# Modulation rows made in thirds, and a row norm whose root is taken on VectorE

## The chip, the cores and the metric

The program runs on one core of a Trainium2 chip. TensorE (PE, with its weight loads PEld), VectorE (DVE), ScalarE (ACT) and GpSimd (POOL) compute; SyncE (SP) issues all DMAs. The metric is the device time of one execution in microseconds, the median of several runs.

## What is computed

Two transformer blocks follow each other on 256 tokens of width 1024; the second block has two layers and, in its first layer, 256 context tokens beside them. All is in 32 bits.

```python
x = x + 0.5 * swiglu(rms_norm(x, ffn1_norm), ffn1_w_in, ffn1_w_out)      # first block
h = rms_norm(x, mix_norm)                                                # RWKV-7 and dilated attention on h @ w_in
x = x + merged @ w_out
x = x + 0.5 * swiglu(rms_norm(x, ffn2_norm), ffn2_w_in, ffn2_w_out)
for l in range(2):                                                       # second block
    ml = split(silu(c) @ w_ada[l] + b_ada[l], 6)                         # six modulation rows of 1024, same for the context
    hl = rmsnorm(xl, norm_g[l, 0]) * (1 + ml[1]) + ml[0]
    yl, yc = mixer(hl, hc, ...)                                          # mLSTM, differential attention, Fourier, merge, w_out
    xl = xl + ml[2] * yl
    xl = xl + ml[5] * swiglu(rmsnorm(xl, norm_g[l, 1]) * (1 + ml[4]) + ml[3], w_ffn_in[l], w_ffn_out[l])
return rmsnorm(xl, final_g)
```

`rms_norm(x, g)` is `x * rsqrt(mean(x*x) + 1e-6) * g`.

## The kernel before

Tokens lie in tiles `X[t]` of 128 rows (t is 0 and 1 for the tokens, 2 and 3 for the context). A product streams its weights through `weights` (L181 to L204): SP loads a 512 KB tile `wr`, ACT casts it to the high part `wh` (L202), DVE takes the low part `wl` (L203), and PE makes three products of each pair (L214 to L216, or L249 to L251 where the weights stand still). Four `wr` and three `wh`/`wl` buffers rotate, so the stream runs a few tiles ahead.

The program is written in one order, and a planner at build time puts each engine's instructions into a list by that order and by its own estimate of when each is ready; later work with its inputs there is pulled ahead into a gap, so an engine's list isn't the written order. On the chip every engine goes through its list in order.

**Modulation.** `ada(l, c0, c1)` makes the columns c0 to c1 of the modulation rows of layer l in steps: a step is 128 rows of `w_ada` by 512 columns (one 256 KB load `wa`, two multiply-adds `aa` on DVE, L1134), eight steps are a chunk, and a chunk is closed by a finish (`finish`, L1114 to L1122): PE sums over the partitions with a column of ones, ACT copies the two rows out, SP writes them to memory. The finish of a chunk is called in the second step of the next one. Four `aa` buffers hold two chunks for both streams. Each weight tile adds `rate` to a counter in `weights`, and each whole unit of it runs one step; what is left of the steps when a feed-forward ends is run there in a loop (`for it in (self.side, self.fine)`). Before, layer 0's 96 steps stand in two halves: 48 in the first feed-forward and 48 in the second of the first block, each at 0.4 a tile over its 66 tiles (the first four tiles of the first feed-forward go by before the generator starts). Layer 1's 96 steps stand in the feed-forward of layer 0, at 1.5 a tile.

**The norm.** `norm_steps` (L334) multiplies a tile by the gain (L338, 1024 columns on DVE); `rms_row` (L326) has ACT sum the squares of the whole row (L330); the mean (L331) and the inverse root (`rsqrt` with n = 1: L286, L290, and three rounds of L292 and L293) go on POOL, nine small instructions one behind the other; DVE then scales each half (L344, or L346 with the shift), PE turns it (L317), and ACT and DVE split it for the next product (L304, L305). `later` queues the second part of a norm, and `tick` and `need` run it between the tiles of a product. The norm of a tile begins when both column halves of its residual (`updates`, L459 or L462 and L463) are added. `outgoing` (L433) runs the last product of a stage, by column halves and groups of tiles, and calls the norm for each group.

**The end.** `last` (L1595): per tile, y = X times gain (L1602), the norm's root on POOL, y times root (L1604), one 512 KB store (L1605).

**Layer 0 of the second block.** `second_layer` (L1520): three branches; after each its gates (`gate_chunk`, eight weight tiles of 4 x 256 for the 1024 columns) and a projection; then `last_projection` with `w_out`, then the feed-forward. The Fourier branch's two products have four weight tiles each. mLSTM and differential attention run inside a pool of their own (`inner`), their gates and all of the Fourier branch outside one.

Of the kernel before, what the change touches and what calls it, by code (L numbers as in the profile page):

```python
# [10 lines left out]
F32 = mybir.dt.float32  # L11
# [120 lines left out]
class Builder:  # L132
    def __init__(self, ctx, tc, a):
# [9 lines left out]
        self.pending, self.credit = [], 0  # L143
# [136 lines left out]
    def rsqrt(self, m, n, name):  # L280

        nc = self.nc
        eng = nc.gpsimd if n == 1 else nc.vector
        y = self.s(n, name + "_y")
        w = self.s(n, name + "_w")
        eng.tensor_scalar(out=y.bitcast(I32), in0=m.bitcast(I32), scalar1=-0.5, scalar2=float(0x5F3759DF),  # L286
                                op0=ALU.mult, op1=ALU.add)
# [38 lines left out]
    def rms_row(self, x, name="rn"):  # L326
        nc = self.nc
        junk = self.q([P, D], F32, "junk")
        ss = self.s(1, name + "_s")
        nc.scalar.activation(out=junk, in_=x, func=AF.Square, accum_out=ss)  # L330
        nc.gpsimd.tensor_scalar(out=ss, in0=ss, scalar1=1.0 / D, scalar2=1e-6, op0=ALU.mult, op1=ALU.add)  # L331
        return self.rsqrt(ss, 1, name)

    def norm_steps(self, xT, t, x, gain, shift):  # L334
# [3 lines left out]
        nc.vector.tensor_tensor(out=hn, in0=x, in1=gain, op=ALU.mult)  # L338
        r = self.rms_row(x)
        yield  # L340
        for c in range(0, D, 512):
            v = hn[:, c:c + 512]
            if shift is None:
                nc.vector.tensor_scalar(out=v, in0=v, scalar1=r[:, 0:1], scalar2=None, op0=ALU.mult)  # L344
            else:
                nc.vector.scalar_tensor_tensor(out=v, in0=v, scalar=r[:, 0:1], in1=shift[:, c:c + 512], op0=ALU.mult,  # L346
                                               op1=ALU.add)
            self.to_split(v, 4, xT, c // P, t)
            yield
# [20 lines left out]
    def ffn(self, X, xT, groups, w_in, w_out, scale, gates, nxt):  # L370
# [9 lines left out]
        for k0, kn in FF_PARTS:  # L380
# [32 lines left out]
            else:  # L413
                self.outgoing(aT, kn, W, groups, res, nxt())
# [18 lines left out]
    def outgoing(self, xT, nk, W, groups, res, done):  # L433


        whole = lambda g: [(t, 0, 512) for t in g]
        if len(groups[0]) > 1:
# [547 lines left out]
    def last_projection(self, yT, nk, W, w, gates, M, first, w_out, groups, res, nxt):  # L985
# [7 lines left out]
        self.outgoing(mT, KD, [[(w_out, 0, c * 512, 512)] for c in range(2)], groups, res, nxt())  # L993

    def first_block(self, X, nxt):
# [17 lines left out]
        def side():  # L1013
# [3 lines left out]
            self.fine, self.rate = self.ada(0, 0, 3 * D), 0.4  # L1017
# [49 lines left out]
        self.last_projection(yT, KD, a["w_proj_rwkv"][0], 256, lambda c0: gate(c0 // 256), M, False, a["w_out"][0], groups,  # L1067
# [3 lines left out]
        with self.inner() as self.ip:  # L1071
            self.fine, self.rate = self.ada(0, 3 * D, 6 * D), 0.4
# [447 lines left out]
    def second_layer(self, l, X, xT, nxt):  # L1520
# [17 lines left out]
        for b, (fn, wb) in enumerate((("mlstm", "w_br_ml_2"), ("diffattn", "w_br_da_2"), ("fourier", "w_br_fn_2"))):  # L1538
            yT = SplitT(self, KD, w)
            if fn == "fourier":  # L1540
                self.fourier(xT, W, outs, yT)
# [4 lines left out]
            gate = lambda c0: [g for c in range(c0, c0 + n, 256) for g in self.gate_chunk(xT, W, U_GATE + b * D + c, w)]  # L1546
            gates = {c0: gate(c0) for c0 in range(0, D, n)}
# [101 lines left out]
```

## Time and profile before

| | us |
|---|---|
| median of 3 runs (2996.62 to 3001.39) | 2996.85 |
| the profiled execution | 3002.16 |
| its span, first to last instruction | 3000.4 |

A busy matmul row lasts longer than it holds up the next one, since matmuls overlap; the distance from one start to the next is what a matmul costs. The granted clock is given as a share of 2.4 GHz: 1.00 is the high level, 0.50 the low one, and values between are windows that saw both. "L" and a number is a line of the kernel. An entry such as [2.45 <-DVE hn L346] is the idle time of the engine just before the instruction and what ended it.

### The profile page before, as it was taken

How to read it: one execution, taken by the hardware profiler on the slowest of the kernel's cores; microseconds unless marked ns; L12 is line 12 of the kernel's file. 1: busy time of each engine (PE TensorE's matmuls, PEld its weight loads, DVE VectorE, ACT ScalarE, POOL GpSimd, SP SyncE). 2: the span in 40 equal slices, each digit the busy share in tenths (PEclk: the TensorE clock that was granted, in tenths of full speed). 3: DMA queues.
4: the chain of work that ended last, by engine and by line, in shares of the span. 5: the costliest groups of instructions: out<-in, count | busy, mean ns of one | idle time of the engine just before them, and what ended most of it. 6: DMA issues, size and time to landing. Idle time of an engine off the chain costs nothing.

```text
span 3000.4 us, 42489 instructions
## 1 busy us (share of the span) xinstructions
PE 2866.2 (96%) x16536; PEld 2436.1 (81%) x16536; DVE 1895.7 (63%) x3228; ACT 1186.0 (40%) x1955; POOL 123.9 (4%) x278
## 2 busy tenths in 40 slices
PE   8988899988998999999999999999999999999998
PEld 7976787777996888987788977877778897799797
DVE  7776958576767455436674266677664555665655
ACT  4434334234443344225442333222344444444443
POOL 1020000002002000000000001000020000000000
PEclk9999979679999999999999999999999999999999
DMA  8766535055674222231233355554442243255564
GB/s 266 222 200 205 169 97 147 32 180 186 211 222 130 67 67 64 75 103 50 64 124 99 88 165 150 159 173 151 155 134 85 85 139 102 78 152 169 168 188 142
DMA packets 298356, 409.59 MB, mean 137 GB/s; under 512 B 31525, under 2 KB 182949, under 8 KB 298154
## 3 DMA queue, kind: packets, MB, share of 16 engines
q1 hardware_dynamic: 298154, 406.87, 44.5%
q8 instruction: 130, 2.13, 0.3%
q14 instruction: 72, 0.59, 0.1%
HBM read 396.98 MB, written 3.24 MB: 133 GB/s over the span
## 4 chain that ended last, share of the span: by engine, by line
PE 80%; DVE 10%; issue 3%; ACT 3%; POOL 2%; DMA 1%; SPq 0%; ACTq 0%; POOLq 0%; DVEq 0%
PE g L215 11%; PE g L216 11%; PE g L214 11%; PE g L249 11%; PE g L251 10%; PE g L250 10%; DVE wl L203 2%; PE dC L1342 2%; PE tr L317 1%; PE I L1318 1%; DVE aa L1134 1%; PE pf L818 1%; ACT dae L1439 1%; PE pf L820 1%; PE f L1509 1%
## 5 line engine op out<-in xcount | busy, mean ns | idle before, releaser
L203 DVE TENSOR_TENSOR wl<-wr,wh 128x1024 fp32r<-128x1024 f32 (+1 forms) x606 | 733.5, 1212 | 630.7 <-ACT wh L202 628.8
L202 ACT CAST wh<-wr 128x1024 fp32r<-128x1024 f32 (+1 forms) x606 | 631.2, 1042 | 1056.2 <-PE g L216 515.6
L215 PE MATMUL g<-wl,xh 128*128 128x512 f32 (+2 forms) x1880 | 733.2, 390 | 13.0 <-DVE wl L203 13.0
L214 PE MATMUL g<-wh,xh 128*128 128x512 f32 (+2 forms) x1880 | 730.0, 391 | 4.4 <-ACT wh L202 2.1
L216 PE MATMUL g<-wh,xl 128*128 128x512 f32 (+2 forms) x1880 | 728.3, 388 | 0.1
L249 PE MATMUL g<-xh,wh 128*128 128x256 f32 (+1 forms) x2352 | 725.9, 309 | 2.2 <-DVE gate L981 1.5
L251 PE MATMUL g<-xh,wl 128*128 128x256 f32 (+1 forms) x2352 | 723.2, 308 | 2.3 <-DVE wl L203 2.3
L250 PE MATMUL g<-xl,wh 128*128 128x256 f32 (+1 forms) x2352 | 722.3, 307 | 0.0
L249 PEld LDWEIGHTS g<-xh,wh 128*128 128x128 f32 x2352 | 452.9, 193 | 33.2 <-issue 7.0
L251 PEld LDWEIGHTS g<-xh,wl 128*128 128x128 f32 x2352 | 453.0, 193 | 25.8 <-DVE wl L203 2.9
L250 PEld LDWEIGHTS g<-xl,wh 128*128 128x128 f32 x2352 | 452.8, 193 | 20.7 <-issue 1.3
L215 PEld LDWEIGHTS g<-wl,xh 128*128 128x128 f32 x1880 | 359.3, 191 | 88.0 <-DVE wl L203 19.5
L214 PEld LDWEIGHTS g<-wh,xh 128*128 128x128 f32 x1880 | 356.6, 190 | 84.1 <-issue 7.5
L216 PEld LDWEIGHTS g<-wh,xl 128*128 128x128 f32 x1880 | 359.4, 191 | 70.5 <-DVE xl L305 1.5
L1134 DVE SCALAR_TENSOR_TENSOR aa<-wa,cond,aa 128x512 f32<-128x512 f32 x336 | 231.9, 745 | 4.8 <-DMA wa<-in_w_ada_dram 4.7
L304 ACT CAST xh<-tr 128x256 fp32r<-128x256 f32 (+1 forms) x114 | 50.4, 463 | 119.8 <-PE tr L317 107.0
L1439 ACT ACTIVATE dae<-sc,dast 128x512 f32<-128x512 f32 (+1 forms) x96 | 58.5, 614 | 42.2 <-DVE dast L1437 37.3
L305 DVE TENSOR_TENSOR xl<-tr,xh 128x256 fp32r<-128x256 f32 (+1 forms) x114 | 57.4, 531 | 18.8 <-ACT xh L304 18.4
L1437 DVE TENSOR_REDUCE dast<-sc 128x1 f32<-128x512 f32 (+1 forms) x96 | 53.8, 597 | 24.2 <-PE sc L1436 23.8
L317 PE MATMUL tr<-ident,hn 128*128 128x128 f32 x160 | 28.5, 315 | 34.1 <-DVE hn L344 17.6
L317 PEld LDWEIGHTS tr<-ident,hn 128*128 128x128 f32 x160 | 22.1, 163 | 43.1 <-DVE hn L344 18.4
L1119 PE MATMUL ada<-aa,one 128*1 128x512 f32 x96 | 30.6, 646 | 27.7 <-DVE aa L1134 27.6
(386 smaller groups left out, 2693.9 us busy)
## 6 DMA issues: line engine op xcount, KB each, us to landing
wr<-in_w_in_dram SPq DMA_DIRECT2D x156, 512.0 KB
wa<-in_w_ada_dram SPq DMA_DIRECT2D x192, 256.0 KB
wr<-in_ffn_w_in_dram SPq DMA_DIRECT2D x88, 512.0 KB
wr<-in_w_ffn_in_dram SPq DMA_DIRECT2D x84, 512.0 KB
wr<-in_w_in_dram SPq DMA_DIRECT2D x156, 256.0 KB
wr<-in_w_ffn_out_dram SPq DMA_DIRECT2D x50, 512.0 KB
wr<-in_ffn_w_out_dram SPq DMA_DIRECT2D x44, 512.0 KB
wr<-in_w_out_dram SPq DMA_DIRECT2D x32, 512.0 KB
```

Source lines behind the costliest of these rows:

```text
L202: nc.scalar.copy(out=wh[:, :kn, :ntot], in_=src)
L203: nc.vector.tensor_tensor(out=wl[:, :kn, :ntot], in0=src, in1=wh[:, :kn, :ntot].bitcast(F32), op=ALU.subtract)
L214: nc.tensor.matmul(o_, xh, wh[:, n0:n1], start=(kc == 0), stop=False)
L215: nc.tensor.matmul(o_, xh, wl[:, n0:n1], start=False, stop=False)
L216: nc.tensor.matmul(o_, xl, wh[:, n0:n1], start=False, stop=(kc == nk - 1))
L249: nc.tensor.matmul(o_, wh[:, fs], xh, start=(kc == 0), stop=False)
L250: nc.tensor.matmul(o_, wh[:, fs], xl, start=False, stop=False)
L251: nc.tensor.matmul(o_, wl[:, fs], xh, start=False, stop=(kc == nk - 1))
L317: self.nc.tensor.transpose(p[:, j * P:(j + 1) * P], src[:, (c + j) * P:(c + j + 1) * P], self.ident)
L1134: nc.vector.scalar_tensor_tensor(out=y, in0=raw, scalar=self.cond[:, k, s:s + 1], in1=acc[s], op0=ALU.mult, op1=ALU.add)
L1342: nc.tensor.matmul(pc[:, 0:257], kw[:, kc * P:(kc + 1) * P], V[t][:, 0:257], start=True, stop=True)
L1439: nc.scalar.activation(out=em, in_=ps[:, 0:n], func=AF.Exp, bias=st[:, m:m + 1], scale=1.0, accum_out=st[:, 2 + m:3 + m])
```

## The change

Layer 0's modulation rows are made in three parts of 32 steps: columns 0 to 2D in the first feed-forward and 2D to 4D in the second, both at 0.6 steps a tile, and 4D to 6D in the Fourier branch and its gates of layer 0, in a pool of their own, at 1.4 a tile, with a loop behind the gates for what is left.

The norm: ACT sums the squares of the first 512 columns as soon as the first column half of the residual is added (`first_half`); DVE squares and sums the other 512, and DVE also takes the root, with the factor -0.5 folded in, so that eight small instructions follow the two sums. With a shift the gain is multiplied in two halves; without one, gain and root go in with one operation per half. The end's store goes out in two halves. In the other branches the gates move inside the pool.

```diff
     def rsqrt(self, m, n, name):
-        eng = nc.gpsimd if n == 1 else nc.vector
...
-        if n == 1:
-            h = self.s(1, name + "_h")
-            eng.tensor_scalar(out=h, in0=m, scalar1=-0.5, scalar2=None, op0=ALU.mult)
-            for _ in range(3):
-                eng.tensor_scalar(out=w, in0=y, scalar1=y[:, 0:1], scalar2=h[:, 0:1], op0=ALU.mult, op1=ALU.mult)
-                eng.tensor_scalar(out=y, in0=w, scalar1=1.5, scalar2=y[:, 0:1], op0=ALU.add, op1=ALU.mult)
-            return y
...
-    def rms_row(self, x, name="rn"):
+    def first_half(self, t, x):
         nc = self.nc
-        junk = self.q([P, D], F32, "junk")
-        ss = self.s(1, name + "_s")
-        nc.scalar.activation(out=junk, in_=x, func=AF.Square, accum_out=ss)
-        nc.gpsimd.tensor_scalar(out=ss, in0=ss, scalar1=1.0 / D, scalar2=1e-6, op0=ALU.mult, op1=ALU.add)
-        return self.rsqrt(ss, 1, name)
+        a = self.sums[t] = self.s(1, "rn_a", bufs=4)
+        nc.scalar.activation(out=self.h([P, 512], F32, "junk"), in_=x[:, 0:512], func=AF.Square, accum_out=a)
+        nc.vector.tensor_scalar(out=a, in0=a, scalar1=-0.5 / D, scalar2=-0.5e-6, op0=ALU.mult, op1=ALU.add)
+
+    def rms(self, t, x, junk):
+        nc = self.nc
+        if t not in self.sums:
+            self.first_half(t, x)
+        a = self.sums.pop(t)
+        h, y, w = self.s(1, "rn_h"), self.s(1, "rn_y"), self.s(1, "rn_w")
+        nc.vector.scalar_tensor_tensor(out=junk, in0=x[:, 512:D], scalar=1.0, in1=x[:, 512:D], op0=ALU.mult,
+                                       op1=ALU.mult, accum_out=h)
+        nc.vector.tensor_scalar(out=h, in0=h, scalar1=-0.5 / D, scalar2=a[:, 0:1], op0=ALU.mult, op1=ALU.add)
+        nc.vector.tensor_scalar(out=y.bitcast(I32), in0=h.bitcast(I32), scalar1=-0.5,
+                                scalar2=float(0x5F3759DF - 0x400000 - 0x40000000), op0=ALU.mult, op1=ALU.add)
+        for _ in range(3):
+            nc.vector.tensor_scalar(out=w, in0=y, scalar1=y[:, 0:1], scalar2=h[:, 0:1], op0=ALU.mult, op1=ALU.mult)
+            nc.vector.tensor_scalar(out=y, in0=w, scalar1=1.5, scalar2=y[:, 0:1], op0=ALU.add, op1=ALU.mult)
+        return y
 
     def norm_steps(self, xT, t, x, gain, shift):
         hn = self.q([P, D], F32, "hn")
-        nc.vector.tensor_tensor(out=hn, in0=x, in1=gain, op=ALU.mult)
-        r = self.rms_row(x)
+        half = lambda v, c: v[:, c:c + 512]
+        if shift is not None:
+            nc.vector.tensor_tensor(out=half(hn, 0), in0=half(x, 0), in1=half(gain, 0), op=ALU.mult)
+        r = self.rms(t, x, half(hn, 512))
+        if shift is not None:
+            nc.vector.tensor_tensor(out=half(hn, 512), in0=half(x, 512), in1=half(gain, 512), op=ALU.mult)
         yield
         for c in range(0, D, 512):
-            v = hn[:, c:c + 512]
+            v = half(hn, c)
             if shift is None:
-                nc.vector.tensor_scalar(out=v, in0=v, scalar1=r[:, 0:1], scalar2=None, op0=ALU.mult)
+                nc.vector.scalar_tensor_tensor(out=v, in0=half(x, c), scalar=r[:, 0:1], in1=half(gain, c), op0=ALU.mult,
+                                               op1=ALU.mult)
...
-    def outgoing(self, xT, nk, W, groups, res, done):
+    def outgoing(self, X, xT, nk, W, groups, res, done):
...
                 for c in range(2):
                     res(g, c, self.gemm(xT, nk, W[c], whole(g)))
+                    if c == 0:
+                        begin(g)
                 done(g)
         else:
             toks = [t for g in groups for t in g]
             res(toks, 0, self.gemm(xT, nk, W[0], whole(toks)))
+            begin(toks)
...
-            self.fine, self.rate = self.ada(0, 0, 3 * D), 0.4
+            self.fine, self.rate = self.ada(0, 0, 2 * D), 0.6
...
-            self.fine, self.rate = self.ada(0, 3 * D, 6 * D), 0.4
+            self.fine, self.rate = self.ada(0, 2 * D, 4 * D), 0.6
...
             if fn == "fourier":
-                self.fourier(xT, W, outs, yT)
+                with self.inner() as self.ip:
+                    if need_ctx:
+                        self.fine, self.rate = self.ada(0, 4 * D, 6 * D), 1.4
+                    self.fourier(xT, W, outs, yT)
+                    gates = {c0: gate(c0) for c0 in range(0, D, n)}
+                    for _ in self.fine:
+                        pass
...
-                    nc.vector.tensor_tensor(out=y, in0=X[t], in1=g, op=ALU.mult)
-                    r = self.rms_row(X[t], "fin")
-                    nc.vector.tensor_scalar(out=y, in0=y, scalar1=r[:, 0:1], scalar2=None, op0=ALU.mult)
-                    nc.sync.dma_start(out=out[0, t * P:(t + 1) * P, :], in_=y)
+                    r = self.rms(t, X[t], y[:, 512:D])
+                    for c in range(0, D, 512):
+                        nc.vector.scalar_tensor_tensor(out=y[:, c:c + 512], in0=X[t][:, c:c + 512], scalar=r[:, 0:1],
+                                                       in1=g[:, c:c + 512], op0=ALU.mult, op1=ALU.mult)
+                        nc.sync.dma_start(out=out[0, t * P:(t + 1) * P, c:c + 512], in_=y[:, c:c + 512])
```

`begin(g)` calls `first_half` for each tile of g.

## Rows read from the trace of the kernel before

**Rows 1.** The page, part 1: busy time of each engine over the whole span.
```profile
PE 2866.2 (96%) x16536; PEld 2436.1 (81%) x16536; DVE 1895.7 (63%) x3228; ACT 1186.0 (40%) x1955; POOL 123.9 (4%) x278
```
**Rows 2.** Windows: length; busy us PE, PEld, DVE, ACT, POOL; clock; DMA; GB/s.
```profile
207.60:238.00 30.40, 8.68 (x28) 2.21 (x28) 25.94 (x40) 6.96 (x13) 14.11 (x19) 0.61 0.52 151
238.00:245.00 7.00, 6.92 (x54) 6.89 (x54) 4.78 (x7) 4.69 (x8) 0.00 (x0) 1.00 0.25 71
909.60:931.70 22.10, 13.58 (x34) 6.22 (x33) 22.10 (x31) 4.84 (x8) 18.98 (x17) 0.77 0.66 214
```
**Rows 3.** The same for the multiply-adds of L1134: VectorE us (count), clock, DMA.
```profile
12.00:204.00 192.00, 44.86 (x64) 1.00 0.76 234
204.00:238.00 34.00, 21.45 (x32) 0.65 0.47 137
...
901.00:932.00 31.00, 21.80 (x32) 0.83 0.68 217
1540.00:1585.00 45.00, 21.72 (x32) 1.00 0.74 229
```
**Rows 4.** Waits of TensorE over the span: who for whom, us, times, longest.
```profile
PE ada L1119 <- DVE aa L1134: 27.6, 3, 13.2
```
**Rows 5.** TensorE in order of time, a finish in a stream: start, length.
```profile
1915.92 0.39 PE L250 MATMUL g<-xl,wh 128*128 128x512 f32 x1
1916.15 0.39 PE L251 MATMUL g<-xh,wl 128*128 128x512 f32 x1
1916.47 1.03 PE L1119 MATMUL ada<-aa,one 128*1 128x512 f32 x4
1917.42 0.50 PE L214 MATMUL g<-wh,xh 128*128 128x512 f32 x1
```
**Rows 6.** In order of time, the norm between w_out and the second feed-forward.
```profile
701.28 0.69 DVE L459 SCALAR_TENSOR_TENSOR X<-g,X 128x512 f32<-128x512 f32 x1 [0.16 <-PE g L216]
...
708.57 1.11 PE L317 MATMUL tr<-ident,hn 128*128 128x128 f32 x4 [5.51 <-DVE hn L344]
```
**Rows 7.** TensorE in order of time, at later norms and at its end.
```profile
1798.67 0.66 PE L317 MATMUL tr<-ident,hn 128*128 128x128 f32 x4 [2.45 <-DVE hn L346]
...
2192.83 1.12 PE L317 MATMUL tr<-ident,hn 128*128 128x128 f32 x4 [2.17 <-DVE hn L346]
...
2794.08 1.12 PE L317 MATMUL tr<-ident,hn 128*128 128x128 f32 x4 [5.98 <-DVE hn L346]
...
2986.85 0.39 PE L216 MATMUL g<-wh,xl 128*128 128x512 f32 x1
```
**Rows 8.** In order of time at the start: first cast, first product.
```profile
9.42 1.05 ACT L202 CAST wh<-wr 128x1024 fp32r<-128x1024 f32 x1 [0.42 <-DMA wr<-in_ffn_w_in_dram]
...
14.42 0.78 PE L214 MATMUL g<-wh,xh 128*128 128x512 f32 x1
```
**Rows 9.** The chain that ended last, its last 16 us: start, length, what.
```profile
2985.08 1.16 ACT junk L330 x2
...
2990.28 0.61 DVE rs L462
...
2996.07 0.76 DVE y L1604
```
**Rows 10.** Groups of VectorE instructions: count, busy, mean, idle before.
```profile
L346 DVE SCALAR_TENSOR_TENSOR hn<-hn,rn_y,mod 128x512 f32<-128x512 f32 x28 | 20.3, 746 | 26.1 <-POOL rn_y L293 26.1
L459 DVE SCALAR_TENSOR_TENSOR X<-g,X 128x512 f32<-128x512 f32 x28 | 18.3, 684 | 1.9 <-PE g L216 1.9
...
L297 DVE SCALAR_TENSOR_TENSOR dars_w<-dars_w,dams 128x4 f32<-128x4 f32 x36 | 5.3, 157 | 0.1
```
**Rows 11.** Windows: Fourier branch, its gates; a VectorE row behind a late load.
```profile
1628.00:1685.00 57.00, 57.00 (x336) 49.70 (x335) 17.35 (x28) 20.80 (x33) 0.00 (x0) 1.00 0.17 48
1685.00:1733.00 48.00, 48.00 (x372) 46.69 (x371) 11.91 (x11) 14.33 (x18) 0.00 (x0) 1.00 0.43 131
...
1558.12 4.73 DVE L1134 SCALAR_TENSOR_TENSOR aa<-wa,cond,aa 128x512 f32<-128x512 f32 x7 [2.67 <-DMA wa<-in_w_ada_dram]
```

More of the change, by code (lines that the diff above doesn't have):

```diff
@@ L282, in rsqrt @@
         nc = self.nc
[L283 removed]
         y = self.s(n, name + "_y")
         w = self.s(n, name + "_w")
[L286 removed]
+        nc.vector.tensor_scalar(out=y.bitcast(I32), in0=m.bitcast(I32), scalar1=-0.5, scalar2=float(0x5F3759DF),
                                 op0=ALU.mult, op1=ALU.add)
[L288 to L294 removed]
         for _ in range(3):
@@ L337, in norm_steps @@
         hn = self.q([P, D], F32, "hn")
-        nc.vector.tensor_tensor(out=hn, in0=x, in1=gain, op=ALU.mult)
-        r = self.rms_row(x)
+        half = lambda v, c: v[:, c:c + 512]
[4 more added lines that the diff above has]
+            nc.vector.tensor_tensor(out=half(hn, 512), in0=half(x, 512), in1=half(gain, 512), op=ALU.mult)
         yield
         for c in range(0, D, 512):
-            v = hn[:, c:c + 512]
+            v = half(hn, c)
             if shift is None:
-                nc.vector.tensor_scalar(out=v, in0=v, scalar1=r[:, 0:1], scalar2=None, op0=ALU.mult)
+                nc.vector.scalar_tensor_tensor(out=v, in0=half(x, c), scalar=r[:, 0:1], in1=half(gain, c), op0=ALU.mult,
+                                               op1=ALU.mult)
             else:
-                nc.vector.scalar_tensor_tensor(out=v, in0=v, scalar=r[:, 0:1], in1=shift[:, c:c + 512], op0=ALU.mult,
+                nc.vector.scalar_tensor_tensor(out=v, in0=v, scalar=r[:, 0:1], in1=half(shift, c), op0=ALU.mult,
                                                op1=ALU.add)
@@ L413, in ffn @@
             else:
-                self.outgoing(aT, kn, W, groups, res, nxt())
+                self.outgoing(X, aT, kn, W, groups, res, nxt())
     def updates(self, X, scale, gates):
@@ L431, in normed, with begin @@
         return xT, done
-    def outgoing(self, xT, nk, W, groups, res, done):
+    def outgoing(self, X, xT, nk, W, groups, res, done):
         whole = lambda g: [(t, 0, 512) for t in g]
+        def begin(g):
+            for t in g:
+                self.first_half(t, X[t])
         if len(groups[0]) > 1:
@@ L983, in project, with last_projection @@
         return range(i0, i0 + len(acc))
-    def last_projection(self, yT, nk, W, w, gates, M, first, w_out, groups, res, nxt):
+    def last_projection(self, X, yT, nk, W, w, gates, M, first, w_out, groups, res, nxt):
         mT = SplitT(self, KD, w)
@@ L992, in last_projection @@
                 self.put_split(mT.dst_span(i * per, per, 0, w), M[i].rearrange("p (k t) -> p k t", t=w))
-        self.outgoing(mT, KD, [[(w_out, 0, c * 512, 512)] for c in range(2)], groups, res, nxt())
+        self.outgoing(X, mT, KD, [[(w_out, 0, c * 512, 512)] for c in range(2)], groups, res, nxt())
     def first_block(self, X, nxt):
@@ L1066, in first_block @@
                     pass
-        self.last_projection(yT, KD, a["w_proj_rwkv"][0], 256, lambda c0: gate(c0 // 256), M, False, a["w_out"][0], groups,
+        self.last_projection(X, yT, KD, a["w_proj_rwkv"][0], 256, lambda c0: gate(c0 // 256), M, False, a["w_out"][0], groups,
                              self.updates(X, 0.5, None), lambda: normed("ffn2"))
@@ L1539, in second_layer @@
             yT = SplitT(self, KD, w)
+            gate = lambda c0: [g for c in range(c0, c0 + n, 256) for g in self.gate_chunk(xT, W, U_GATE + b * D + c, w)]
             if fn == "fourier":
-                self.fourier(xT, W, outs, yT)
+                with self.inner() as self.ip:
[5 more added lines that the diff above has]
+                        pass
             else:
@@ L1545, in second_layer @@
                     getattr(self, fn)(xT, W, l, outs, yT)
-            gate = lambda c0: [g for c in range(c0, c0 + n, 256) for g in self.gate_chunk(xT, W, U_GATE + b * D + c, w)]
-            gates = {c0: gate(c0) for c0 in range(0, D, n)}
+                gates = {c0: gate(c0) for c0 in range(0, D, n)}
             if b < 2:
@@ L1554, in second_layer @@
             res = self.updates(X, 0.5, {s: self.mod_row(l, s, 2) for s in streams})
-            self.last_projection(yT, KD, a[wb][l], w, gates.get, M, False, a["w_out_2"][l], groups, res, ffn_norm)
+            self.last_projection(X, yT, KD, a[wb][l], w, gates.get, M, False, a["w_out_2"][l], groups, res, ffn_norm)
         gates = {s: self.mod_row(l, s, 5) for s in streams}
```

2 lines of the change are left out of this document (1 added, 1 removed).

## The prediction, written before the change was run

> **What bounds the kernel now.** I read the page's busy shares first: TensorE is busy 96% of the span, VectorE 63%, GpSimd 4% [rows 1]. A step therefore pays only where TensorE stands still or runs at its low clock. The list of waits has one entry far above the rest: 27.6 us behind the modulation multiply-adds, in three waits [rows 4]. The windows then show the two long holes [rows 2]. From 207.6 to 238 us (between the first feed-forward and the mixer) TensorE is busy 8.7 of 30.4 us at a granted clock of 0.61, while VectorE is busy 25.9; from 909.6 to 931.7 (between the first block and mLSTM) it runs at 0.77 and VectorE is busy all 22.1 us. VectorE's work there is the tail of the modulation steps: 32 multiply-adds, 16 steps, in each hole [rows 3]. Last I read the norms, each by itself in order of time: at each the transposes wait for a root on GpSimd [rows 6 to 9].
>
> **Why the tail is 16 steps.** From the code: a finish is called in the second step of the next chunk, so finishes are calls 10, 18, 26 and so on; the buffers let VectorE run two chunks ahead of the last finish. In the first feed-forward, 62 tiles at 0.4 give 24.8 calls, so two finishes fall inside, four chunks (32 steps) can run, and two are left over. The trace agrees: 64 multiply-adds, 32 steps, up to 204 us, and 32 behind it [rows 3].
>
> **Thirds: what they take away.** At 0.6 a tile, 33 calls end on tile 59 of 66 in the first feed-forward (4 + 33/0.6) and on tile 55 in the second. Neither has anything left, and the first carries 32 steps in the stream as it did before, so its VectorE load doesn't grow.
>
> First hole. From 207.6 to 245.0 us, 37.4 us, TensorE's own work is 48 products of 288 columns and 16 transposes, which the filled window prices at 7.0/54 = 0.13 us each [rows 2]: 64 x 0.13 = 8.3. Lost: 29. What is late next is the second tile's norm: residual 0.68, squares 0.75, root, scaling, transposes and split, some 5 us, of which token tile 0's 24 products (3.1 us) cover the larger part. I leave 2 us there and take 27.
>
> Second hole. In its 22.1 us TensorE made 24 products of 512 columns by the code's order, at 0.23 from start to start [rows 5], 5.5 us. Lost: 16.6. Next in line are the context tiles' products, whose norms are long done: another 24 of them, 5.5 us, before the normed tokens are needed. I take 16.5.
>
> **Thirds: what they add.** Of layer 0's twelve finishes seven lay in the holes, where TensorE had nothing else. Now all lie in streams. In a stream the next product starts 1.27 us after the last one instead of 0.23 [rows 5], and one more start is 0.1 late: 1.15 each, 8 us in all.
>
> The last 32 steps go to the Fourier branch: 32 loads on SP's queue in front of weight loads, 64 multiply-adds of 21.72/32 = 0.68 us (43 us) on VectorE, eight small copies on ACT, small fills on POOL, which nobody awaits. The cover: layer 1's first 16 steps were pulled ahead into 1540 to 1585 us before [rows 3], with TensorE full; the same place should take 16 of the new ones, and layer 1's 16 move behind. For the other 16, VectorE is free 39.7 of 57 us in the branch and 36.1 of 48 in the gates [rows 11], against 21.7 us of work. But 16 tiles at 1.4 are 22 calls of 33: two finishes fall in, and the third and fourth are left to the loop behind the gates. Two finishes let all 32 steps run, so that only the finishes should be late. I take 2 us; if the last 11 steps weren't pulled ahead, they would cost what the first hole did per step, 30.4/16 x 11 = 21.
>
> **The norm.** Per tile, GpSimd's nine instructions go; VectorE gets squares over 512 columns and nine small ones. For the squares no row exists: the nearest are 0.684 and 0.746 us for 512 columns [rows 10], and a read of the sum may come on top, as ACT has one; I take 0.75, with 0.95 as the upper end. A small one takes 0.157 [rows 10] and may start closer to the one before: the eight that follow cost 0.8 to 1.3. With the gain in halves, a shifted tile costs VectorE about 0.75 + 1.05 = 1.8 us more, an unshifted one less, since its gain is merged: at most 40 us over 22 tiles, which VectorE's idle third hides; uncovered, all of it would be on the path. The wait that is added is VectorE's for ACT's half sum; behind it stand residuals and `wl`, but that sum is asked for one column half earlier, four weight tiles before. The gates that move into the pools are the same instructions in the same order; I cost them at nothing.
>
> The row of line L346, an operation of this form with two operands of 32 bits from SBUF, takes 0.746 us against 0.684 for L459, whose one operand is in PSUM [rows 10]: 9% more. The Trainium skill (Vector Engine (DVE) Microarchitecture Reference, section 7) says that this form with two such sources runs at half rate, because both read ports are taken and none is left to read back the accumulator, which speaks against putting the squares here. By it each squaring would take an estimated 1.4 us at most (twice 0.68), and the eight on the path would give back 5 us of the sum, 49 in place of 54; the row, which has no accumulator, doesn't show it.
>
> On the path, place by place:
> - Start: the first product begins at 14.42, held by the POOL root; the first cast weights are there at 9.42 + 1.05 = 10.5 [rows 8], so up to 4 us; I take 3.
> - Between w_out and the second feed-forward: the residual ends at 701.97, transposes begin at 708.57 after 5.51 us idle [rows 6]. Now 0.75 + 1.3 + 0.75 us: begin at 704.8, 3.8 earlier. I take 3.5.
> - Layer 0's norms in front of its feed-forward: one wait of 2.45 [rows 7]; pulled-ahead steps of layer 1 may now stand there. I take 2.
> - In front of layer 1's mixer: two waits of this kind, one at each pair of tiles, 2.17 shown [rows 7]. I take 4.5.
> - In front of the last feed-forward: 5.98 [rows 7]; 2 to 3 us of the chain stay. I take 3.5.
> - The end: the first tile's ACT and POOL chain from 2985.08 holds VectorE, so the second residual, whose products ended at 2987.2 [rows 7], starts only at 2990.28; y ends at 2996.83 [rows 9]. Now: 2985.06 + 0.75 + 1.3 + 1.5 = 2988.6, residual 1.3, then 3.4 again: 2993.3. I take 3.5, and 0.5 for the smaller last store: 4.
>
> Together 20.5.
>
> **Sum.** 27 + 16.5 - 8 - 2 + 20.5 = 54. The profiled execution took 3002.16 us, span 3000.4 and 1.8 around it: 2948. It lies 5.3 above the median run, so the median comes to 2997 - 54 = **2943**.
>
> **Rivals.**
> - *The chain is no shorter on VectorE.* In GpSimd's list nothing stood between the nine instructions; in VectorE's the planner may put a `wl` or a residual between any two; three of 0.68 us [rows 10] bring 1.3 + 0.75 back to the old 4. Against: the end has nothing to put in, the start little. Only 7 of the 20.5 stay: 2957. Chance 0.22.
> - *The Fourier third leaves a tail of its own*, as worked out above, 21 instead of 2: 2962. For: 22 calls of 33. Against: two finishes inside. Chance 0.12.
> - *The tails don't go*, because the last chunk still waits for its finish: half of the 43.5 stays, 2965. Against: the count of calls, which fits the trace. Chance 0.05.
> - *Slower: loads laid bare in the Fourier branch.* There the steps share SP's queue with a stream that reads little, and if VectorE takes a step's multiply-adds as soon as its load is issued, it waits for each landing with `wl` behind it: 2.67 us of idle in such a row [rows 11], and TensorE starves. 32 x 2.67 = 85 us against 54 gained: 3028. It decides from 21 bare steps on. Against: only two such waits among the 16 steps pulled ahead before. Chance 0.06.
>
> **How the numbers follow.** The forecast has 0.53, unnamed mixtures 0.02. Low end: every norm at its bound (4 + 3.8 + 2.5 + 4.5 + 6 + 4, some 25), the holes whole (29 + 16.6), less 0 to 8 for finishes: 2997 - 63 to 71, so 2926. The high end takes in the first three rivals and a norm part that gives little: 2969. Faster by over 0.2% (6 us, about what a measurement of this kernel can tell from no change): 0.92; slower: 0.06; within: 0.02.
>
> **What would show it.** Right: no modulation row behind 200 us up to the second feed-forward; the mixer's first product 2 to 5 us after the last of the feed-forward; mLSTM's stream unbroken at clock 1.00; VectorE rows for the root and no POOL ones; TensorE still full from 1600 to 1735 us; a last y some 4 us nearer to the last matmul. Wrong: `wl` or residual rows between the root's rows with transposes still idle for 4 us or more; multiply-adds in a block behind the gates with TensorE waiting; VectorE idle for `wa` between 1540 and 1735 us; or waits for `wl` in the first feed-forward.

## The result, and the profile after

The changed kernel took **2961.28 us** (four executions, 2954.22 to 2967.27) against 2996.73 before: ratio 0.9878, interval 0.9849 to 0.9907. It is faster by 35.5 us, inside the range of 2926 to 2969, but the gain is two thirds of the 54 us forecast. Run once more beside its predecessor it took 2964.23 against 2999.04, ratio 0.9894 (0.9879 to 0.9909).

The two profiled executions compared below are 3002.16 and 2966.07 us, 36.1 apart. Page, part 1, of the changed kernel (busy us, share, instructions), which answers [rows 1]:

```profile
PE 2860.1 (96%) x16536; PEld 2433.6 (82%) x16536; DVE 1933.1 (65%) x3478; ACT 1176.9 (40%) x1955; POOL 22.4 (1%) x81
```

VectorE took over 37 us of work, GpSimd lost 101. TensorE's busy time fell by 6 us, its idle time by 30. The list of waits of TensorE led with the modulation before [rows 4]; its next entries for normed tokens (`hn`) and weight rests (`wl`, the low part of a weight tile) were, before (us in total, times, longest):

```profile
PE tr L317 <- DVE hn L344: 17.6, 3, 11.9
PE tr L317 <- DVE hn L346: 16.5, 7, 6.0
PE g L215 <- DVE wl L203: 13.0, 8, 5.6
```

Now the list begins:

```profile
PE g L215 <- DVE wl L203: 21.9, 12, 5.2
PE tr L309 <- DVE hn L357: 17.5, 3, 10.0
PE tr L309 <- DVE hn L360: 6.8, 1, 6.8
```

The modulation is gone from it. The waits for normed tokens fell from 34.1 to 24.3 us (10.0 of these are the start of the run), and the waits for weight rests rose from 13.0 to 21.9: nearly all that was gained on the one was lost on the other. The windows at the two holes and at what follows them (length; busy us PE, PEld, DVE, ACT, POOL; clock; DMA; GB/s), to be read against [rows 2]:

```profile
207.30:221.00 13.70, 11.05 (x66) 9.58 (x66) 11.27 (x26) 5.98 (x9) 0.00 (x0) 0.88 0.42 123
221.00:228.00 7.00, 7.00 (x33) 5.79 (x32) 3.46 (x3) 3.12 (x4) 0.00 (x0) 1.00 0.95 275
885.00:907.00 22.00, 22.00 (x109) 17.75 (x108) 15.48 (x33) 6.80 (x10) 0.00 (x0) 1.00 0.32 96
```

The second hole is wholly filled at clock 1.00. Of the first, one wait in front of the transposes and some low clock are left. The windows of the modulation's instructions (PE finishes, weight loads, VectorE multiply-adds), against [rows 3]:

```profile
14.00:200.00 186.00, 4.11 (x16) 0.37 (x16) 44.55 (x64) 1.00 0.73 228
200.00:700.00 500.00, 0.00 (x0) 0.00 (x0) 23.06 (x32) 0.86 0.47 146
700.00:870.00 170.00, 5.12 (x16) 0.45 (x16) 22.36 (x32) 1.00 0.62 196
870.00:1500.00 630.00, 0.00 (x0) 0.00 (x0) 0.00 (x0) 0.99 0.24 74
1500.00:1583.00 83.00, 0.00 (x0) 0.00 (x0) 21.70 (x32) 1.00 0.54 174
1583.00:1760.00 177.00, 3.94 (x16) 0.46 (x16) 41.67 (x61) 1.00 0.48 156
```

Where the 36 us come from shows when the same instruction is looked up in both traces and the distance (after less before) is followed along the run. Points are TensorE's starts, on VectorE ends; distances are taken from the unrounded times:

| point | before | after | distance | change of distance | forecast of the step |
|---|---|---|---|---|---|
| first product | 14.4 | 11.8 | -2.6 | start 2.6 gained | 3 |
| last product, first feed-forward | 207.2 | 207.0 | -0.2 | two more finishes 2.4 lost | (in 8) |
| first product in the mixer behind both token tiles | 279.7 | 256.1 | -23.6 | first hole 23.4 gained | 27 |
| last transposes of the mixer's attention | 636.9 | 613.8 | -23.1 | 0.5 lost | - |
| an activation in the second feed-forward (VectorE) | 726.9 | 700.1 | -26.8 | norm after w_out 3.7 gained | 3.5 |
| last residual there (VectorE) | 906.3 | 882.6 | -23.8 | finishes 3.0 lost | (in 8) |
| first transposes in mLSTM | 944.3 | 902.5 | -41.8 | second hole 18.0 gained | 16.5 |
| first product in the Fourier branch | 1627.6 | 1587.0 | -40.6 | 1.2 lost | - |
| first residual behind the gates (VectorE) | 1780.2 | 1744.0 | -36.1 | Fourier third 4.5 lost | 4 finishes of the 8, and 2 |
| last finish, layer 1's modulation | 2166.9 | 2128.8 | -38.1 | layer 0's norms 2.0 gained | 2 |
| last gate product, layer 1's mLSTM | 2237.6 | 2204.0 | -33.6 | layer 1's mixer norm **4.5 lost** | 4.5 gained |
| last product of all | 2986.9 | 2953.5 | -33.4 | last feed-forward's norm 0.2 lost | 3.5 gained |
| end of the span | 3000.4 | 2964.3 | -36.1 | end 2.7 gained | 4 |

By this the thirds brought 31.5 of 33.5 us (23.4 + 18.0 - 2.4 - 3.0 - 4.5), the norm 6.3 of 20.5. This split goes by place: what the shorter norm does inside the two holes counts with the thirds. One caution for all that follows: two profiles of this same kernel differ by 5.9 us in span, and their distance goes from +0.2 at 210 to -5.7 at 570 us, in the mixer, where TensorE drops in and out of its low clock (window 300 to 580: mean granted clock 0.82 in the first, 0.84 in the second). Much of the 13 us between executions should come from there, and a difference there is not put down to an edit.

### The profile page after: what moved, and what is told of

Read it like the earlier page. It is cut to its first block, busy times and chain, and to the rows that moved or that the text cites. A ratio compares the mean times of both kernels' runs of the same rounds, so it can differ in the third digit from the quotient of the medians.

```text
span 2964.3 us, 42526 instructions
## 1 busy us (share of the span) xinstructions
PE 2860.1 (96%) x16536; PEld 2433.6 (82%) x16536; DVE 1933.1 (65%) x3478; ACT 1176.9 (40%) x1955; POOL 22.4 (1%) x81
## 5 line engine op out<-in xcount | busy, mean ns | idle before, releaser
L215 PE MATMUL g<-wl,xh 128*128 128x512 f32 (+2 forms) x1880 | 731.2, 389 | 21.9 <-DVE wl L203 21.9
L309 PE MATMUL tr<-ident,hn 128*128 128x128 f32 x160 | 27.0, 307 | 24.3 <-DVE hn L357 17.5
L1364 PE MATMUL dC<-vo,kw 128*128 128x257 f32 x192 | 50.3, 395 | 0.0
L1156 DVE SCALAR_TENSOR_TENSOR aa<-wa,cond,ab 128x512 f32<-128x512 f32 x48 | 34.9, 746 | 20.1 <-PE ada L1141 16.7
```

Of the source, the lines that this page charges most:

```text
L215: nc.tensor.matmul(o_, xh, wl[:, n0:n1], start=False, stop=False)
L1156: nc.vector.scalar_tensor_tensor(out=y, in0=raw, scalar=self.cond[:, k, s:s + 1], in1=acc[s], op0=ALU.mult, op1=ALU.add)
L1364: nc.tensor.matmul(pc[:, 0:257], kw[:, kc * P:(kc + 1) * P], V[t][:, 0:257], start=True, stop=True)
```

## The experiments

**The changed kernel once more.** No edit.

> The changed kernel once more, as it is. Its first four executions lay between 2954.2 and 2967.3 us, so one profile of it may mix terms of two courses. Theory A (one course, some spread): median 2958 to 2964, and the profile shows the same terms as the first one within 1 us each. Rival B (two courses about 10 us apart): some executions near 2955 and some near 2966, and where the profile is one of 2955 us one stretch of it is 8 to 10 us shorter than in the first one, the others equal.

2964.23 us (2960.11 to 2969.67), span of the profile 2958.3. It is one course with a spread, A, except that the spread has a place: the mixer, as above. The waits of the list agree with the first profile within 1.1 us in each entry.

**The thirds alone**, with norms as before:

```diff
-            self.fine, self.rate = self.ada(0, 0, 3 * D), 0.4
+            self.fine, self.rate = self.ada(0, 0, 2 * D), 0.6
...
-            self.fine, self.rate = self.ada(0, 3 * D, 6 * D), 0.4
+            self.fine, self.rate = self.ada(0, 2 * D, 4 * D), 0.6
...
+                    if need_ctx:
+                        self.fine, self.rate = self.ada(0, 4 * D, 6 * D), 1.4
```

> The kernel before with the modulation rows in thirds alone; norms, factors and the last store as before. Theory A (the terms add up): the first trace gives the holes 23.7 + 17.4 us, less 2.3 + 3.0 + 4.5 for finishes in the three streams and 2.4 in mixer and mLSTM: 29 gained, 2968 us; the layer-1 norm waits stay at about 4.6 us in all, as in the trace before. Rival B (the 4.5 us lost in front of layer 1's mixer come from the modulation steps that now lie elsewhere): the loss shows here too, 24 gained, 2973 us.

2972.80 us, ratio 0.9921 (0.9907 to 0.9936): 26 us gained, between A and B. But B's mechanism is not there. TensorE's waits in front of layer 1's mixer (2100 to 2230 us) are as before the change, where they were 4.6 and 0.4 us (2150 to 2240 us):

```profile
PE tr L317 <- DVE hn L346: 4.8, 3, 2.4
PE g L215 <- DVE wl L203: 0.2, 1, 0.2
```

So what layer 1 loses comes with the norm. The holes give less here, 20.5 and 13.4 us against 23.4 and 18.0 with both changes: once the tail is gone, TensorE waits there for the norm, 2.8 and 2.0 us with the old one, 2.4 and nothing with the new.

**The norm alone**, the modulation in halves as before (the diff above, backwards, on the changed kernel):

> The changed kernel with the modulation rows in halves as before: the norm's change alone. Theory A (the root on VectorE gives in some places and takes in others): start 2.6, norm after w_out 3.7, layer 0's feed-forward norm 2, end 2.7 gained, 4.5 lost in front of layer 1's mixer, nothing in front of the last feed-forward: 6 gained, 2991 us. Rival B (the norm is worth what was forecast, and the thirds took it): 15 to 20 gained, 2977 to 2982 us.

2995.26 us, ratio 0.9986 (0.9977 to 0.9995): 3.8 gained, as A says, nowhere near B. 26.2 and 3.8 make 30; together the two gave 34.8 on the same chip. The intervals alone would allow such a difference, but the traces show an interplay of that sign at the second hole, where the norm in VectorE's list meets the tail of multiply-adds that was left there. VectorE has hardly a gap there, and the norm's 22 new rows, 5.4 us long, stand among the multiply-adds and weight rests for which TensorE waits. TensorE in the kernel before (first two rows) and in this one:

```profile
917.24 2.52 PE L1119 MATMUL ada<-aa,one 128*1 128x512 f32 x4 [5.93 <-DVE aa L1134]
926.80 0.80 PE L215 MATMUL g<-wl,xh 128*128 128x512 f32 x1 [2.55 <-DVE wl L203]
...
906.75 2.53 PE L1141 MATMUL ada<-aa,one 128*1 128x512 f32 x4 [9.59 <-DVE aa L1156]
915.17 0.80 PE L215 MATMUL g<-wl,xh 128*128 128x512 f32 x1 [5.90 <-DVE wl L203]
```

Against the kernel before, this kernel's distance goes from -14.2 to -8.7 us across that hole. The thirds take the tail away, and with it this loss of 5.5.

**The root's eight small operations on GpSimd**, the rest of the change as it is:

```diff
-        nc.vector.tensor_scalar(out=h, in0=h, scalar1=-0.5 / D, scalar2=a[:, 0:1], op0=ALU.mult, op1=ALU.add)
+        eng = nc.gpsimd
+        eng.tensor_scalar(out=h, in0=h, scalar1=-0.5 / D, scalar2=a[:, 0:1], op0=ALU.mult, op1=ALU.add)
...
```

> The changed kernel with the eight small operations of the root on GpSimd; squares by halves, thirds and merged factors stay. Theory A (on VectorE the root stands in front of weight rests, on GpSimd it runs beside them): TensorE's waits for weight rests in front of layer 1's mixer, 7.9 us in three waits, fall below 1 and the 4.5 us come back; start, norm after w_out and end get 1 to 1.5 us longer each: about 4 faster than the changed kernel, 2957 us. Rival B (not the root but the squares or the residuals hold the weight rests up): the waits stay and the exposed norms get longer: 2965 us.

2980.17 us, ratio 0.9935 (0.9922 to 0.9948): 16 slower than the changed kernel, so both forecasts fall. A's mechanism exists: in front of layer 1's mixer the waits for rests go from 7.9 to 5.5 us and 2.9 us come back. But the other norms lose 2 to 5 each. At the start the list has tile 1's first operation ahead of tile 0's second, so GpSimd stands idle for tile 1's load, and the first product begins at 15.69 instead of 11.8:

```profile
8.99 0.27 POOL L335 TENSOR_SCALAR rn_h<-rn_h,rn_a 128x1 f32<-128x1 f32 x1 [3.70 <-DVE rn_a L323]
```

Later GpSimd's operations are held up by VectorE's long ones. GpSimd and VectorE of this kernel around 2191 us:

```profile
2191.88 2.25 POOL L340 TENSOR_SCALAR rn_w<-rn_y,rn_h 128x1 f32<-128x1 f32 x1
2194.23 0.27 POOL L341 TENSOR_SCALAR rn_y<-rn_w,rn_y 128x1 f32<-128x1 f32 x1
2194.60 0.34 POOL L340 TENSOR_SCALAR rn_w<-rn_y,rn_h 128x1 f32<-128x1 f32 x1
...
2191.64 2.36 DVE L203 TENSOR_TENSOR wl<-wr,wh 128x1024 fp32r<-128x1024 f32 x2
```

The same operation takes 0.34 us and, begun under two weight rests, 2.25: until these end.

**The weight rests kept out of one root**: in the last feed-forward's norm the next eight rests are ordered behind token tile 0's root.

```diff
+            if self.held:
+                self.held -= 1
+                self.tc.add_manual_dep(rest.ins, self.root,
+                                       mybir.DependencyInfo(mybir.DependencyClass.NoSync, mybir.DependencyReason.DATA))
```

> The changed kernel, but in the last feed-forward's norm the next eight weight rests on VectorE are ordered behind the first token tile's root (an order on one engine, no wait). In the changed kernel two rests of 1.21 us lie between that root's rows. Theory A (what is put between the root's rows eats the gain of VectorE's shorter root): TensorE's wait of 6.8 us in front of that feed-forward falls by 2 to 2.4 to about 4.5, and the time by 2: 2962 us where the changed kernel has 2964. Rival B (the rests are needed at once behind the transposes): the wait goes over to the rests, and the time stays.

2961.53 us, ratio 0.9892 (0.9875 to 0.9908): not to be told from the changed kernel. No rest lies between that root's rows any more, and the wait falls from 6.77 to 5.76 us, half of what A says. Then it is given back, and 1.1 us more (distance to the repeated changed kernel -1.5 ahead of this place, -0.4 behind it). TensorE and VectorE of this kernel:

```profile
2753.29 1.12 PE L314 MATMUL tr<-ident,hn 128*128 128x128 f32 x4 [5.76 <-DVE hn L367]
...
2751.36 1.22 DVE L204 TENSOR_TENSOR wl<-wr,wh 128x1024 fp32r<-128x1024 f32 x1
2752.49 0.75 DVE L367 SCALAR_TENSOR_TENSOR hn<-hn,rn_y,mod 128x512 f32<-128x512 f32 x1
2753.15 2.35 DVE L204 TENSOR_TENSOR wl<-wr,wh 128x1024 fp32r<-128x1024 f32 x2
...
2757.23 0.75 DVE L367 SCALAR_TENSOR_TENSOR hn<-hn,rn_y,mod 128x512 f32<-128x512 f32 x1
```

Of the two rests that stood in the root (at 2757.43 and 2758.69 us of the changed kernel), one now stands between the root's last row and the first half's factor at 2752.49, still ahead of the transposes, and two more ahead of the second half's factor at 2757.23. One rest of 1.2 us left the chain, and the wait fell by 1.0: A's mechanism, at about its price per rest. For the time it is B: the rests are due at once, and wherever they stand, something on the path stands behind them. What the wait would be with no rest in the chain, this run doesn't show.

**The rests of the second pair earlier**, at the output projections in pairs of token tiles:

```diff
+            with self.tc.high_priority(offset=self.ahead):
...
+                    self.ahead = 400 if g == groups[1] else 0
```

> The changed kernel, but in front of layer 1's mixer (and at the other feed-forward and output projections in pairs of token tiles) the planner may put the weight rests of the second pair earlier, ahead of and between the root's rows of the first pair. Theory A (there the rest is late because the root's rows stand in front of it): TensorE's three waits for weight rests, 7.9 us between 2110 and 2210 us, fall below 3, and 3 to 5 us come back: 2960 us. Rival B (the same work in another order: the first pair's factors are late instead): the wait moves to the transposes and the time stays within 1 us.

2961.64 us, ratio 0.9889 (0.9871 to 0.9907). The waits of TensorE from 2100 to 2215 us:

```profile
PE g L217 <- DVE wl L205: 9.5, 2, 9.3
PE tr L311 <- DVE hn L362: 0.7, 1, 0.7
```

Three waits of 7.9 us have become one of 9.3. Against the repeated changed kernel the trace gains 6.8 us up to 2160 and has given all of it back by 2168, at that one wait. That is B: the same work in another order. The windows say why there was nothing to win: of the 44 us from 2131 to 2175, VectorE is busy 43.23 in this kernel and 41.88 in the repeated changed one. In the kernel before, at the same place (2174 to 2218), it was 35.45.

**The refinement left out** (six of the root's eight small operations):

```diff
-        for _ in range(3):
-            nc.vector.tensor_scalar(out=w, in0=y, scalar1=y[:, 0:1], scalar2=h[:, 0:1], op0=ALU.mult, op1=ALU.mult)
-            nc.vector.tensor_scalar(out=y, in0=w, scalar1=1.5, scalar2=y[:, 0:1], op0=ALU.add, op1=ALU.mult)
```

> The changed kernel with the three refinement rounds of every norm's root left out (six of its eight small operations; the root is then the first estimate alone). Theory A (the root's length is on the path at each exposed norm): a dependent small operation takes 0.28 us from start to start, six take 1.7; exposed are the start, the norms after w_out, in front of both mixers and both second-layer feed-forwards, and two at the end, seven or eight places: 11 to 14 us faster than the changed kernel, 2950 to 2953 us. Rival B (only the place of rests and residuals in VectorE's list counts): under 4 us, above 2960.

2942.30 us, ratio 0.9824 (0.9809 to 0.9839): 21 us faster than the changed kernel, beyond A and far from B. Against the repeated changed kernel the distance grows by 1.5 to 2 us at the mixer, after w_out, at mLSTM and at the last feed-forward, by about 5 and 5.5 at the two places with pairs of token tiles (1720 to 1790 and 2140 to 2180) and by 2.9 at the end. A priced one root at each place, 1.7 us. That fits where one tile's root is waited for; the places with pairs have four roots, on a VectorE with little room, and the end has two. TensorE's wait in front of the last feed-forward, 6.77 us in the changed kernel:

```profile
2737.01 0.66 PE L309 MATMUL tr<-ident,hn 128*128 128x128 f32 x4 [3.08 <-DVE hn L357]
```

This wait fell by 3.7 us, more than six operations last, because the two rests that stood between the root's rows now stand behind the first factor. So the run shortens the root and reorders the list at once, and doesn't tell the two apart place by place.

**Each finish's products made twice**, in both layers:

```diff
-            for o, x in zip(at, acc):
+            for o, x in list(zip(at, acc)) * 2:
```

> The changed kernel with the column sums' products of all 24 finishes (12 of each layer) made twice. Theory A (a finish in a stream costs TensorE the time of its products, 0.95 to 1.05 us): 23 to 25 us slower than the changed kernel, 2987 to 2989 us, spread over the streams. Rival B (a finish costs its wait and the change-over, not its products): under 10 us, below 2975.

2980.51 us, ratio 0.9942 (0.9922 to 0.9962): 16 slower than the changed kernel; 20 by the two profiles. Against the repeated kernel's trace it lags by 0.87 to 0.89 us more at each finish, some 21 us for the 24. (The lag reaches 24.0 us at the last of them, but 4.9 of that come up in the first block's mixer, where no finish lies, and aren't put down to the edit.) 3.7 us fall back at layer 1's mixer norm, where VectorE was the later one. A's mechanism is borne out at a price a little below its range; its total isn't.

**No Fourier third** (these rows of the modulation are only a copy of the second third's):

```diff
-                        self.fine, self.rate = self.ada(0, 4 * D, 6 * D), 1.4
+                        nc.sync.dma_start(out=self.mod[0][:, 4 * D:6 * D], in_=self.mod[0][:, 2 * D:4 * D])
```

> The changed kernel without the last third of layer 0's modulation: its rows are copied from the second third, so no steps run in the Fourier branch. Theory A (of the Fourier third only its four finishes are late): 3.5 to 4.5 us faster than the changed kernel, about 2959 to 2960 us, all of it between 1590 and 1760 us. Rival B (it crowds VectorE and pushes layer 1's first steps into worse places): over 8 us, 2956 or less, part of it behind 1760 us.

2956.53 us, ratio 0.9858 (0.9843 to 0.9872), against 0.9894 and 0.9878 of the changed kernel: 6 to 11 faster. By the traces 7.1 us come between 1540 and 1790 us; 2.7 are lost just ahead, from 1530 to 1540, and 1.7 go back later, so that 2.7 are left. The other 6 us or so of the difference arose far ahead of this place, most of it in the first block's mixer, and aren't put down to the edit. So the time doesn't decide between A and B. In the stretch itself the four finishes (3.9 us of products) and some 3 us that look like crowding of VectorE were saved; the crowding isn't shown by itself. The leftover steps, which the prediction feared, cost nothing that shows: 29 multiply-adds lie between 1693 and 1760 us, and TensorE is busy 66.94 of those 67 us.

**Two refinement rounds**, and **both last edits that speed up the norm**:

```diff
-        for _ in range(3):
+        for _ in range(2):
             nc.vector.tensor_scalar(out=w, in0=y, scalar1=y[:, 0:1], scalar2=h[:, 0:1], op0=ALU.mult, op1=ALU.mult)
```

> The changed kernel with two refinement rounds in a norm's root in place of three (its relative error is then a few millionths). Theory A (every dependent small operation lies on the path at the exposed norms): a third of the 20 to 22 us that leaving all three rounds out gave, 6.6 to 7.3: 2955 to 2957 us. Rival B (the gain of the short root came from the last two operations that stand behind the weight rests, or from the rests' new order): not a third; either under 3 or over 11.

> Two refinement rounds, and the weight rests of the second pair of token tiles earlier, both as in the runs before. If the two add up: 7 + 2 faster than the changed kernel, 2954 us; if the earlier rests now only change places with a shorter root: as with two rounds alone, 2956 to 2957.

Two rounds took 2956.83 us, ratio 0.9863 (0.9849 to 0.9878), 4 to 9 us less than the two measurements of the changed kernel (its interval overlaps that of the first and ends just below that of the second): A's third of what leaving all rounds out gave, as far as the spread lets one say. With the rests earlier as well it is 2959.68, ratio 0.9869 (0.9853 to 0.9885). They don't add up; against two rounds alone its trace gains 6 us up to 2160 and loses 7 up to 2220. Of the kernels that compute everything, two rounds alone has the lowest median, at a slightly coarser root; its interval overlaps those of the next ones.

## Why the prediction was right in its range and wrong in its size

**What bounds, and the holes: right.** The two holes are filled. The first gave 23.4 us of 27: the wait for the norm was the 2 us forecast (2.42), but the sum had priced all 64 instructions at the filled window's 0.13 us, and the first eight products run at the lower clock, 0.24 to 0.41 us apart, after eight transposes that take 1.55. TensorE behind the first feed-forward:

```profile
206.98 0.39 PE L216 MATMUL g<-wh,xl 128*128 128x512 f32 x1
209.79 1.90 PE L309 MATMUL tr<-ident,hn 128*128 128x128 f32 x8 [2.42 <-DVE hn L357]
211.34 0.59 PE L214 MATMUL g<-wh,xh 128*128 128x288 f32 x1
```

The mixer's first product comes 4.4 us after the last one before it, inside the 2 to 5 named as the sign. The sign "no modulation row behind 200 us" was badly put: 32 multiply-adds stand between 200 and 700, the second feed-forward's first steps pulled ahead under a busy TensorE, as the planner had done before.

**The finishes: right in total.** 8 us and 2 us for the Fourier leftovers were forecast, 9.9 found in the three streams, and the doubled products put the price of the products at 0.87 to 0.89 us each. The parts fit less well: 2.4 us for two more finishes in the first stream, 3.0 for one more in the second (where another is split over two places, 787 and 812 us), 4.5 for four in the Fourier branch. The 2 us went to finishes and to what looks like crowding, not to leftovers.

**The norm: the step that failed.** 20.5 us were forecast, 6.3 found in the trace, 3.8 measured alone and 8.6 on top of the thirds. Of the 14.2 us that the trace lacks, 9.0 are missing in front of layer 1's mixer, 3.7 in front of the last feed-forward, 1.3 at the end and 0.4 at the start; after w_out and in layer 0 the sum came out. The step that failed is to count each wait for normed tokens as gained and VectorE's new rows as hidden: where VectorE has no room, TensorE waits for a weight rest instead. In front of layer 0's feed-forward 4.9 us of waits for normed tokens (1798 and 1828 us) became 3.6 for rests (1764 to 1791), in front of layer 1's mixer 4.6 became 7.7. The prediction's own sign of being wrong showed as well, rests and residuals between the root's rows with transposes idle for over 4 us (5.09 after w_out, 6.77 in front of the last feed-forward). The norm's terms, one by one:

- *The squares* were sized rightly: 0.75 forecast, 0.69 and a read of 0.08 measured. Groups of VectorE instructions (count, busy, mean ns, idle before), beside L346 in [rows 10]:

```profile
L360 DVE SCALAR_TENSOR_TENSOR hn<-hn,rn_y,mod 128x512 f32<-128x512 f32 x28 | 20.2, 743 | 0.1
L339 DVE TENSOR_SCALAR rn_w<-rn_y,rn_h 128x1 f32<-128x1 f32 x66 | 16.8, 267 | 0.8
L340 DVE TENSOR_SCALAR rn_y<-rn_w,rn_y 128x1 f32<-128x1 f32 x66 | 12.9, 208 | 0.7
L332 DVE SCALAR_TENSOR_TENSOR hn<-X 128x512 f32<-128x512 f32 x14 | 9.5, 687 | 5.7 <-DMA X<-in_x_dram 5.6
```

The half rate that the Trainium skill (Vector Engine (DVE) Microarchitecture Reference, section 7) gives for this form with two 32-bit SBUF sources is not seen: the squares, whose two sources are the same tile, are faster with an accumulator (687 ns) than the factors without one (743).

- *The small operations* were mis-sized. "A small one takes 0.157 and may start closer to the one before: 0.8 to 1.3" used a row of another form, and a duration where the spacing counts. With tiles as scalars they take 0.21 and 0.27, and one that needs the last one's output starts 0.19 to 0.31 after it. The last norm, with nothing between its rows:

```profile
2956.84 0.68 DVE L332 SCALAR_TENSOR_TENSOR y<-X 128x512 f32<-128x512 f32 x1
2957.46 0.08 DVE L332 DVE_READ_ACCUMULATOR y<-X 128x1 f32 x1
2957.57 0.21 DVE L334 TENSOR_SCALAR rn_h<-rn_h,rn_a 128x1 f32<-128x1 f32 x1
2957.82 0.15 DVE L336 TENSOR_SCALAR rn_y<-rn_h 128x1 int32<-128x1 int32 x1
2958.01 0.27 DVE L339 TENSOR_SCALAR rn_w<-rn_y,rn_h 128x1 f32<-128x1 f32 x1
2958.32 0.21 DVE L340 TENSOR_SCALAR rn_y<-rn_w,rn_y 128x1 f32<-128x1 f32 x1
...
2959.68 1.42 DVE L1632 SCALAR_TENSOR_TENSOR y<-X,rn_y,fg 128x512 f32<-128x512 f32 x2
```

From 2957.57 to 2959.68 are 2.1 us for the eight, 0.8 to 1.3 more than forecast. That the root's length costs time was shown, as without six of the eight 21 us are gone; how much of the missing 14.2 is this price, and how much is what stands between and behind the rows, wasn't measured separately.

- *The rival "the chain is no shorter on VectorE"* came nearest (2957, 7 of the 20.5 left). Its mechanism was seen behind w_out, where two weight rests and a residual lie between the rows and the root takes 4.55 us (679.56 to 684.11), so that TensorE's wait is 5.09 where it was 5.51 [rows 6]:

```profile
679.69 1.22 DVE L203 TENSOR_TENSOR wl<-wr,wh 128x1024 fp32r<-128x1024 f32 x1
680.82 0.14 DVE L336 TENSOR_SCALAR rn_y<-rn_h 128x1 int32<-128x1 int32 x1
680.89 0.68 DVE L481 SCALAR_TENSOR_TENSOR X<-g,X 128x512 f32<-128x512 f32 x1
681.48 0.26 DVE L339 TENSOR_SCALAR rn_w<-rn_y,rn_h 128x1 f32<-128x1 f32 x1
681.66 1.21 DVE L203 TENSOR_TENSOR wl<-wr,wh 128x1024 fp32r<-128x1024 f32 x1
682.80 0.20 DVE L340 TENSOR_SCALAR rn_y<-rn_w,rn_y 128x1 f32<-128x1 f32 x1
...
684.96 1.97 PE L309 MATMUL tr<-ident,hn 128*128 128x128 f32 x8 [5.09 <-DVE hn L357]
```

The wait fell by 0.4 where 3.8 were worked out. The 3.7 us gained there come mostly from what follows: some 2 of them because TensorE is back at its full clock (starts 0.23 us apart instead of 0.43) after three products instead of eight, the rest at shorter waits behind the second tile. That 3.5 were forecast is luck. In the last feed-forward the same mechanism stands in the rows (two rests and a residual in the root); ordering the rests behind it there took one of them out of the chain, which returned 1 us of the wait and nothing of the time, while a shorter root returned time at every place.

- *Layer 1's mixer* had the wrong sign: 4.5 us forecast as a gain, 4.5 lost. The working counted the wait for normed tokens alone [rows 7] and not who stands behind the new rows on VectorE. There the two tiles' roots run interleaved from 2147.8 to 2153.6, and the rest of a weight tile whose cast was done at 2149.8 waits among them:

```profile
2152.29 1.22 DVE L203 TENSOR_TENSOR wl<-wr,wh 128x1024 fp32r<-128x1024 f32 x1
...
2149.83 0.73 PE L214 MATMUL g<-wh,xh 128*128 128x512 f32 x2 [0.73 <-ACT wh L202]
2153.56 0.80 PE L215 MATMUL g<-wl,xh 128*128 128x512 f32 x1 [2.99 <-DVE wl L203]
...
2179.45 0.68 PE L215 MATMUL g<-wl,xh 128*128 128x512 f32 x1 [4.68 <-DVE wl L203]
```

"VectorE's idle third hides it" was an average; at this place VectorE is busy 17.44 of 20 us. The other experiments fit: with the root on GpSimd 2.9 us came back, without the refinement 5.5, with the thirds alone the loss is absent, and with the rests earlier the wait moved, on a VectorE that is busy 43.23 of 44 us.

- *The end* gave 2.7 of 4; the root's extra 0.8 to 1.3 us is as much as is missing.

**The other rivals.** The Fourier third left no tail, the tails of the holes did go, and no loads were laid bare in the Fourier branch.

## What to carry to other kernels

Price a chain of dependent small operations by the start-to-start spacing of such a chain with the same kinds of operands, not by the duration of a lone row, and count every such chain on the path: 0.13 us in the price of one operation, times eight operations and some eight places, makes an estimated 8 us here. When work moves to a busier engine, ask at each place who stands behind it in that engine's list: a wait that is taken away can come back as a wait for something else, here for weight rests. An engine's mean share says nothing of the places that matter. Before moving a root to a faster engine, ask whether it needs all its rounds.

## What the runs showed of the hardware

- Small GpSimd operations stood still under VectorE's two-source SBUF operations: 0.34 us alone, 2.25 us under two weight rests, ending as these ended. The Trainium skill (SBUF — State Buffer, SBUF: two separate sides) says that the two engines share a port pair that one of them holds for a whole instruction; the rows agree: the small operation, begun 0.24 us after the first rest, ended 0.13 us after the second. This is one cause that the trace shows for the 16 us by which the root on GpSimd was slower; the other is the order of its list at the start, 3.9 us.
- A [128x1] operation that depends on the one before it starts 0.19 to 0.31 us after it on VectorE; on GpSimd, undisturbed, the spacing is 0.29 to 0.44.
- With identical instructions the spans of two executions differ by 6 us, nearly all of it where TensorE's granted clock goes up and down in the mixer (0.82 against 0.84 over 280 us).
